# Planning a whole kernel with the scheduler's detailed time model, with TensorE held to the order of the source

## The chip, the cores and the metric

The kernel runs on one core of a Trainium2 chip. The metric is the device time of one execution in microseconds (us), lower is better. The core has five engines that work beside each other, each of which takes its own instructions in a fixed order: TensorE (PE, with its weight loads shown as PEld), VectorE (DVE), ScalarE (ACT), GpSimd (POOL) and SyncE (SP, which only issues DMAs). ACT and POOL issue some DMAs too.

## What is computed

One layer of an encoder on 2048 tokens of width 1024: a gated linear attention mixer (GLA), then a feed-forward network with a short causal convolution, each behind an RMS norm and with a residual sum, and a last RMS norm.

```python
def gla_mixer(h, w_in, w_gate2, b_gate, norm_w, w_out):
    q, k, v, r, glr = split(h @ w_in)                  # 4 heads, dk 128, dv 256, gate rank 16
    log_a = log_sigmoid(glr @ w_gate2 + b_gate) / 16
    g = cumsum(log_a within chunks of 64); g_end = g[:, :, -1]
    k_dec = k * exp(g_end - g)
    # over the chunks: state = state * exp(g_end) + k_dec^T v ;  o = q state
    o = rms_normalize(o) * norm_w * silu(r)
    return o @ w_out

def conv_ffn(h, w_up, conv_w, conv_b, w_down):
    u = causal_dwconv(h @ w_up, conv_w, conv_b)        # 3 taps, 2 x 2816 channels
    g, val = split(u, 2)
    return (silu(g) * val) @ w_down

def reference(x, ...):
    x = x + gla_mixer(rmsnorm(x, mix_norm_w), ...)
    x = x + conv_ffn(rmsnorm(x, ffn_norm_w), ...)
    return rmsnorm(x, final_norm_w)
```

## The kernel before

**Arithmetic.** Everything is fp32 at full precision: each operand is split into a rounded part and a rest (`split`: ACT makes `hi` at line 193, DVE makes `lo` at line 194), and each product takes three matmuls of 128x128 weights against 512 columns (`mm3p`, lines 184 to 186). Each large matrix product is done in seven block products p1 to p7 instead of eight (a Strassen-Winograd scheme), which is why sums and differences of blocks are made, stored to HBM and read again.

**Stages.** They follow one another in the source:

- R, A, B: the input projections, in 8 pairs of token tiles each (`unit`). R makes the gate r and the gates' pre-activations; A and B make q, k, v of two heads each. The gates (`gates`, lines 606 to 654) run beside R and the beginning of A: a pre-activation, softplus, split, a prefix sum by matmul (`pd`, line 639), an exponential on ACT (line 640), a store, and a transpose of the result on TensorE (`pe`, line 631). The scan over chunks runs in slots between the products of A and B and at the beginning of Y: `scan_f` (transposes `pq`, silu of r at line 714), `scan_k` (state update, `pk`), `scan_o` (`po`, then the normalized row `og` at line 763), `scan_x` (transposes `px` of og, line 771).
- Y: the mixer's output projection, the residual sum, the second norm, and the transposes of its rows, h2 (`blocks`, `pt_d`, line 840).
- The up-projection with convolution (`phase_u`): 2 halves of the tokens, each with 11 groups of two channel tiles and all seven products. POOL forms weight sums (lines 1274 to 1292), ACT and DVE split them (`uw`), TensorE multiplies (`ua`, `ub`, `uc`), ACT copies results out of PSUM (`c`, lines 1297 and 1411), ACT and DVE do the convolution (lines 1313 and 1315), and the results go to HBM. h_p are the split operands, read from HBM as `hz` (first half) and `hd` (second half).
- The down-projection: 7 products in 2 halves (`pd_p`, weights `dw`, activations `da` read from HBM), the last sums and the norm.

**What sets the order.** The source is one straight program of 15,608 traced instructions, counting pool markers. It emits work in an order that its author has laid out: a small clock in the program (`adv`, `later_do`) places the preparation of later products, the gates, the scan and the transposes among the products of the present one, with delays such as TB0 to TB3 in microseconds. After that the compiler's planner orders each engine's instructions: it runs the program on a model of the chip and, whenever an engine is free in that model, gives it the earliest instruction in source order among those that the model has ready. An engine's order therefore differs from the source's wherever the model has an earlier instruction waiting. Buffers are rotating slots of fixed number; an instruction that writes a slot waits for the slot's last reader. A few order edges are written by hand (`issue_after`): they hold an instruction behind another one of the same engine, without a wait for its end.

```python
    def mm3p(ps_ap, pairs, first=True, last=True, more=False, mid=None):
        for i, ((ah, al), (bh, bl)) in enumerate(pairs):
            nc.tensor.matmul(ps_ap, ah, bl, start=(first and i == 0), stop=False, **kw)   # 184
            nc.tensor.matmul(ps_ap, al, bh, start=False, stop=False, **kw)                # 185
            nc.tensor.matmul(ps_ap, ah, bh, start=False, stop=..., **kw)                  # 186
            adv(3 * 0.227 * ps_ap.free_size() / 512)
            ...
    def split(hi, lo, src):
        order["act"] = nc.scalar.copy(hi, src)                                            # 193
        nc.vector.tensor_sub(lo, src, f32(hi))                                            # 194
```

Other lines that the profile names: 461 multiplies the transposed input `xt` by the norm's weight (`hb`) on DVE; 1069, 1154 and 1211 take projection results out of PSUM (`cp` is the ACT copy of the first product of a bank); 226 and 828 belong to the second norm (`var_d`, the store of `x1d`).

Of the kernel before, what the change touches and what calls it, by code (L numbers as in the profile page):

```python
# [22 lines left out]


@with_exitstack
def hybrid_kernel(
    ctx: ExitStack,
    tc: tile.TileContext,
    x: bass.AP,
# [1607 lines left out]
            use(o, s, m, banks[m], nwf)  # L1637


_INS = [  # L1640
    "x", "xt", "mix_norm_w", "ffn_norm_w", "final_norm_w",
    "gla_w_in", "gla_w_gate2", "gla_b_gate", "gla_norm_w", "gla_w_out",
# [35 lines left out]
```

## Time and profile before

| | us |
|---|---|
| median of 3 runs | 2118.95 (2118.75 to 2119.75) |
| the profiled execution's own time | 2119.17 |
| its span, first to last instruction | 2117.5 |
| PE busy | 2049.1 |
| DVE busy | 1605.2 |
| ACT busy | 1109.4 |
| POOL busy | 672.5 |

The mean granted clock of TensorE is 0.994. A busy time is the union of an engine's instructions; matmuls overlap a little in it, since one record is about 0.39 us long while the next begins after about 0.23 us. An engine's idle time before an instruction is put down to whatever ended it; idle time matters where it holds up the engine that bounds a stage. Times in rows count from the start of the span.

### The profile page before, as it was taken

How to read it: one execution, taken by the hardware profiler on the slowest of the kernel's cores; microseconds unless marked ns; L12 is line 12 of the kernel's file. 1: busy time of each engine (PE TensorE's matmuls, PEld its weight loads, DVE VectorE, ACT ScalarE, POOL GpSimd, SP SyncE). 2: the span in 40 equal slices, each digit the busy share in tenths (PEclk: the TensorE clock that was granted, in tenths of full speed). 3: DMA queues.
4: the chain of work that ended last, by engine and by line, in shares of the span. 5: the costliest groups of instructions: out<-in, count | busy, mean ns of one | idle time of the engine just before them, and what ended most of it. 6: DMA issues, size and time to landing. Idle time of an engine off the chain costs nothing.

```text
span 2117.5 us, 28200 instructions
## 1 busy us (share of the span) xinstructions
PE 2049.1 (97%) x9700; PEld 1686.1 (80%) x9700; DVE 1605.2 (76%) x2109; ACT 1109.4 (52%) x2022; POOL 672.5 (32%) x595
## 2 busy tenths in 40 slices
PE   6999999999998998999999999999999999999998
PEld 4777778878886887888888887888888788888886
DVE  7766887888878646899898867898898956566564
ACT  5656755675665666655545545445454533233342
POOL 2110000000000002555464554666766433243310
PEclk9999999999999999999999999999999999999999
DMA  8866675577858888444545376545445684454462
GB/s 293 295 219 199 223 237 178 165 247 254 292 183 267 314 271 293 155 159 136 182 139 167 132 278 204 140 110 152 122 129 148 196 322 155 144 179 164 148 218 112
DMA packets 246512, 419.32 MB, mean 198 GB/s; under 512 B 22784, under 2 KB 91520, under 8 KB 246368
## 3 DMA queue, kind: packets, MB, share of 16 engines
q1 hardware_dynamic: 203200, 335.09, 46.5%
q10 hardware_dynamic: 36832, 70.89, 9.8%
q0 software_dynamic: 6336, 11.54, 3.5%
q8 instruction: 76, 1.25, 0.2%
q14 instruction: 68, 0.56, 0.1%
HBM read 278.50 MB, written 150.47 MB: 203 GB/s over the span
## 4 chain that ended last, share of the span: by engine, by line
PE 64%; DVE 13%; POOL 7%; issue 7%; DMA 7%; ACT 2%; SPq 0%; ACTq 0%; DVEq 0%; POOLq 0%
PE pd_p L184 7%; PE pd_p L186 7%; PE pd_p L185 7%; DVE t L1315 4%; PE ua L185 4%; PE ua L184 4%; PE ua L186 3%; POOL as_p L1344 3%; DVE uw_p L194 3%; PE mp_A L184 2%; PE mp_Y L184 2%; PE mp_Y L185 2%; PE mp_Y L186 2%; PE mp_A L185 2%; PE mp_A L186 2%
## 5 line engine op out<-in xcount | busy, mean ns | idle before, releaser
L184 PE MATMUL ua<-h_p,uw_p 128*128 128x512 f32 x704 | 276.9, 393 | 10.2 <-ACT c L1297 4.5
L185 PE MATMUL ua<-h_p,uw_p 128*128 128x512 f32 x704 | 276.0, 392 | 2.8 <-DVE var_d L226 2.8
L186 PE MATMUL ua<-h_p,uw_p 128*128 128x512 f32 x704 | 275.5, 391 | 0.0
L1315 DVE SCALAR_TENSOR_TENSOR t<-u,cw,t 128x1024 f32<-128x1024 f32 x176 | 265.6, 1512 | 8.5 <-ACT t L1313 7.8
L184 PE MATMUL pd_p<-dw_p,da 128*128 128x512 f32 x616 | 239.6, 389 | 0.0
L185 PE MATMUL pd_p<-dw_p,da 128*128 128x512 f32 x616 | 239.6, 389 | 0.0
L186 PE MATMUL pd_p<-dw_p,da 128*128 128x512 f32 x616 | 239.6, 389 | 0.0
L193 ACT CAST uw_p<-us 128x512 fp32r<-128x512 f32 x132 | 82.2, 622 | 198.8 <-POOL us L1277 138.3
L194 DVE TENSOR_TENSOR da<-da_p,da 128x512 fp32r<-128x512 f32 x154 | 118.9, 826 | 87.9 <-ACT da L193 87.9
L194 DVE TENSOR_TENSOR uw_p<-us,uw_p 128x512 fp32r<-128x512 f32 x132 | 153.3, 1166 | 42.4 <-ACT uw_p L193 37.7
L194 DVE TENSOR_TENSOR uw_p<-ur,uw_p 128x512 fp32r<-128x512 f32 x176 | 146.3, 860 | 28.1 <-ACT uw_p L193 28.1
L184 PEld LDWEIGHTS ua<-h_p,uw_p 128*128 128x128 f32 x704 | 133.0, 189 | 43.2 <-ACT c L1297 8.9
L193 ACT CAST da<-da_p 128x512 fp32r<-128x512 f32 x154 | 84.7, 618 | 150.4 <-PE pd_p L186 115.3
L185 PEld LDWEIGHTS ua<-h_p,uw_p 128*128 128x128 f32 x704 | 133.0, 189 | 30.6 <-DVE uw_p L194 3.4
L186 PEld LDWEIGHTS ua<-h_p,uw_p 128*128 128x128 f32 x704 | 133.2, 189 | 27.9
L760 POOL TENSOR_TENSOR rstd<-var,pair 128x2 f32<-128x2 f32 x32 | 22.7, 709 | 410.7 <-DVE var L759 410.7
L184 PE MATMUL uc<-h_p,uw_p 128*128 128x512 f32 x352 | 137.1, 390 | 1.2 <-DMA h_p<-hd_p 1.2
L186 PE MATMUL uc<-h_p,uw_p 128*128 128x512 f32 x352 | 137.0, 389 | 0.0
L185 PE MATMUL uc<-h_p,uw_p 128*128 128x512 f32 x352 | 136.9, 389 | 0.0
L1313 ACT ACTIVATE t<-u,cw 128x1024 f32<-128x1024 f32 x88 | 109.6, 1245 | 49.9 <-DVE u L1424 49.1
L186 PEld LDWEIGHTS pd_p<-dw_p,da 128*128 128x128 f32 x616 | 115.6, 188 | 24.1
L185 PEld LDWEIGHTS pd_p<-dw_p,da 128*128 128x128 f32 x616 | 115.6, 188 | 24.1
(263 smaller groups left out, 5287.3 us busy)
## 6 DMA issues: line engine op xcount, KB each, us to landing
ur<-in_ffn_w_up_dram SPq DMA_DIRECT2D x84, 512.0 KB, 5.2
da_p<-ad_p SPq DMA_DIRECT2D x154, 256.0 KB, 4.1
ad_p<-t SPq DMA_DIRECT2D x110, 256.0 KB, 3.1
ch<-in_ffn_w_down_dram SPq DMA_DIRECT2D x61, 256.0 KB, 4.9
hr_A_p<-h1d_p SPq DMA_DIRECT2D x56, 256.0 KB, 3.3
hr_B_p<-h1d_p SPq DMA_DIRECT2D x56, 256.0 KB, 3.2
hr_Y_p<-yd_p SPq DMA_DIRECT2D x56, 256.0 KB, 3.9
hd_p<-h2p_p ACTq DMA_DIRECT2D x56, 256.0 KB, 2.1
```

Of the source, the lines that this page charges most:

```text
L184: nc.tensor.matmul(ps_ap, ah, bl, start=(first and i == 0), stop=False, **kw)
L185: nc.tensor.matmul(ps_ap, al, bh, start=False, stop=False, **kw)
L186: nc.tensor.matmul(ps_ap, ah, bh, start=False, stop=(last and i == len(pairs) - 1), **kw)
L193: order["act"] = nc.scalar.copy(hi, src)
L194: nc.vector.tensor_sub(lo, src, f32(hi))
L760: nc.gpsimd.tensor_tensor(rstd, var, neghalf.to_broadcast([P, 2]), op=ALU.pow)
L1313: nc.scalar.activation(t, u[:, 2:2 + TS], AF.Identity, scale=cw[:, 2, c:c + 1], bias=cw[:, 3, c:c + 1])
L1315: nc.vector.scalar_tensor_tensor(t, u[:, k:k + TS], cw[:, k, c:c + 1], t, op0=ALU.mult, op1=ALU.add)
L1344: upool["ins"] = nc.gpsimd.tensor_add(av, last if x is None else x, y)
```

## The change

The body of the kernel is renamed, and a new outer function runs all of it inside one block of the tile context. The block is to be planned with the compiler's more detailed model of the chip's timing instead of the usual one, and inside it TensorE is set to manual scheduling: its instructions keep the order of the source, and the planner chooses only for the other engines and their DMA queues. No instruction of the body, no buffer and no hand-written order edge is touched.

```diff
 @with_exitstack
-def hybrid_kernel(
+def body(
     ctx: ExitStack,
     tc: tile.TileContext,
     x: bass.AP,
...
             use(o, s, m, banks[m], nwf)
 
 
+def hybrid_kernel(tc, *args):
+    with tc.block(schedule_with_timeline_sim=True):
+        with tc.manual_schedule(engines={mybir.EngineType.PE}):
+            body(tc, *args)
+
+
 _INS = [
```

## Prediction

> **What bounds the kernel now.** I read the page first, then the stretches by stage, then what TensorE (PE) waits for, and last the order of time around each of its long waits.
>
> ```profile
> span 2117.5 us, 28200 instructions
> PE 2049.1 (97%) x9700; PEld 1686.1 (80%) x9700; DVE 1605.2 (76%) x2109; ACT 1109.4 (52%) x2022; POOL 672.5 (32%) x595
> ...
> 25.00:295.00 270.00, 256.49 (x1359) 207.01 (x1358) 200.86 (x304) 173.22 (x334) 34.74 (x56) 1.00 0.72 239
> 295.00:660.00 365.00, 349.89 (x1936) 290.24 (x1935) 295.35 (x572) 225.62 (x498) 19.75 (x28) 0.99 0.68 226
> ...
> 870.00:1210.00 340.00, 338.90 (x1494) 280.09 (x1493) 304.41 (x311) 179.51 (x274) 169.46 (x141) 1.00 0.47 156
> 1300.00:1660.00 360.00, 357.45 (x1569) 293.48 (x1568) 317.54 (x281) 178.09 (x263) 243.28 (x187) 1.00 0.47 127
> 1720.00:2090.00 370.00, 370.00 (x1634) 306.39 (x1633) 217.84 (x285) 128.03 (x232) 107.31 (x80) 1.00 0.53 184
> ```
>
> After each stretch's length come the busy times of PE, PEld, DVE, ACT and POOL, then granted clock, DMA share and GB/s. The matmuls are the bound: PE is idle for 2117.5 - 2049.1 = 68.4 us in all. The up-projection (870 to 1210, 1300 to 1660) leaves it 1.1 and 2.6 us idle, the down-projection none. The idle time lies in the mixer's stages, 13.5 us (25 to 295) and 15.1 us (295 to 660), and at the head, the two seams of the feed-forward part and the tail. No instruction's work changes, so a new order can win at most that idle time and the halved clock that follows some of it.
>
> Four places show a fault of order: an engine that takes its instructions in order stands at one whose input has not come, with ready work for PE behind it. A row has start, length, engine, line, operation and tiles, and in brackets the engine's idle time and what ended it. The landing row is that of tile xt in the first 16 us; a row with an arrow from engine to engine gives a wait's total, count and longest.
>
> ```profile
> 8.99 2.50 DVE L194 TENSOR_TENSOR w_R_p<-ws_p,w_R_p 128x1024 fp32r<-128x1024 f32 x2 [7.31 <-ACT w_R_p L193]
> DMA to landing us min/median/max: 2.8/6.6/8.0
> 12.93 1.29 DVE L461 TENSOR_TENSOR hb<-xt,nwt 128x512 f32<-128x512 f32 x2
> 14.73 0.79 PE L184 MATMUL m_R<-w_R_p,h_R 128*128 128x512 f32 x1 [14.73 <-ACT h_R L193]
> ...
> 311.87 0.63 ACT L714 ACTIVATE r<-r 128x512 f32<-128x512 f32 x1 [3.25 <-DMA r<-rd]
> 312.40 0.67 ACT L1211 ACTIVATE cp_A<-mp_A,rs 128x512 f32<-128x512 f32 x1
> 313.13 0.51 PE L184 MATMUL mp_A<-w_A_p,h_A_p 128*128 128x512 f32 x1 [1.95 <-ACT cp_A L1211]
> ...
> PE mp_A L184 <- ACT cp_A L1211: 2.7, 3, 1.9
> ...
> 828.38 2.23 ACT L193 CAST h_p<-h_p 128x1024 fp32r<-128x1024 f32 x2 [0.56 <-DMA h_p<-hz_p]
> 830.52 1.13 ACT L193 CAST uw_p<-ur 128x512 fp32r<-128x512 f32 x2
> 831.18 1.02 PE L184 MATMUL ua<-h_p,uw_p 128*128 128x512 f32 x2 [3.09 <-ACT uw_p L193]
> 834.97 0.79 PE L185 MATMUL ua<-h_p,uw_p 128*128 128x512 f32 x1 [2.77 <-DVE var_d L226]
> ...
> 1670.81 0.62 ACT L193 CAST da<-da_p 128x512 fp32r<-128x512 f32 x1 [1.05 <-DMA da_p<-ad_p]
> ...
> 1671.96 0.61 PE L184 MATMUL ua<-h_p,uw_p 128*128 128x512 f32 x1 [2.48 <-ACT c L1411]
> ```
>
> At 311.87 ACT waited 3.25 us for a gate row; the copy that frees PE's bank (cp_A) stood behind it. At 828 and 1670 it is the same with h_p and da. The planner must have expected those landings sooner. There are three waits for cp_A, 2.7 us in all.
>
> **The change part by part.**
>
> *The block* adds a jump at either end for every engine; nothing hides the first. No row shows its price. The nearest is what now lies around the span for entry and exit, 2119.17 - 2117.5 = 1.7 us; I bound it by 0 and that and take the middle, 0.8.
>
> *TensorE held to the source's order.* I set the matmuls in the order in which the source emits them against their order in the trace: 395 of 9700 stand elsewhere, in 20 places, nearly all where the gates end and the scan begins (226 to 256 us), where stages B and Y begin, and at the transposes of h2. At each the planner let ready products go ahead of an operation whose input was late; pinned, PE waits there.
>
> ```profile
> 238.11 0.39 PE L184 MATMUL mp_A<-w_A_p,h_A_p 128*128 128x512 f32 x1
> ...
> 240.31 0.66 PE L631 MATMUL pe<-ident,e 128*128 128x128 f32 x4
> ...
> 242.68 0.39 PE L639 MATMUL pd<-ll,later 128*128 128x512 f32 x1
> ...
> 244.42 0.48 PE L639 MATMUL pd<-ll,later 128*128 128x512 f32 x1
> ...
> 248.41 0.66 PE L631 MATMUL pe<-ident,e 128*128 128x128 f32 x4
> 248.82 0.48 PE L639 MATMUL pd<-ll,later 128*128 128x512 f32 x1
> ...
> 250.76 0.60 PE L631 MATMUL pe<-ident,e 128*128 128x128 f32 x4
> ...
> 428.91 0.39 PE L184 MATMUL mp_B<-w_B_p,h_B_p 128*128 128x512 f32 x1
> ...
> 432.19 0.41 PE L771 MATMUL px<-ident,og 128*128 128x128 f32 x2
> ...
> 642.41 0.39 PE L184 MATMUL mp_Y<-w_Y_p,h_Y_p 128*128 128x512 f32 x1
> ...
> 646.23 0.41 PE L771 MATMUL px<-ident,og 128*128 128x128 f32 x2 [0.93 <-DVE og L763]
> ...
> 658.89 0.90 PE L771 MATMUL px<-ident,og 128*128 128x128 f32 x3 [4.91 <-DVE og L763]
> ```
>
> Scan start: the source puts the pe of 240.31 where the product of 238.11 stands, so PE waits 2.2 us; then pd (242.68) follows at once instead of behind six products, some 1.7 more. Later pe, pd, pe stand together, and each pe needs the exponential of the pd before it: 3.9 us from 244.42 to 248.41 as now, 1.9 from 248.82 to 250.76 at best; less what lies between, 1.2 to 3.9 and 1.3 to 1.9. Sum 6.4 to 9.7; I take 8.0, most of the way up, since these latencies belong to ACT and DVE.
>
> What absorbs part of the rest, and what idle time costs in clock:
>
> ```profile
> 310.70:317.20 6.50, 4.55 (x14) 3.25 (x13) 4.53 (x9) 3.68 (x8) 0.00 (x0) 0.74 0.52 190
> 827.70:840.00 12.30, 6.42 (x17) 4.37 (x16) 8.72 (x11) 7.87 (x12) 6.76 (x5) 0.72 1.01 409
> PE mp_B L185 <- DVE h_B_p L194: 2.0, 2, 1.8
> PE px L771 <- DVE og L763: 7.0, 3, 4.9
> PE mp_Y L185 <- DVE h_Y_p L194: 1.4, 1, 1.4
> ```
>
> Start of B: the transpose px moves from behind eleven products to ahead of them: 432.19 - 428.91 = 3.3 us, against the wait of 1.8 and the third px wait (7.0 - 4.9 - 0.9 = 1.2), both within the next 25 us, which a later PE no longer meets: +0.3. Start of Y: 646.23 - 642.41 = 3.8, less the 0.9 there, the 1.4 behind it, and 2.7 of the 4.9 at 658.89, which twelve products now fill (12 x 370/1634 us, the pace of the down-projection): -1.2. The h2 transposes pass seven products in one place and six in another, 1.6 + 1.4 = 3.0. A later PE asks nothing of SP's or POOL's queues.
>
> Around the 1.95 us wait at 313 the granted clock is 0.74 over 6.5 us, so (1 - 0.74) x 6.5 = 1.7 us of matmul are lost; around the seam at 831 it is 0.28 x 12.3 = 3.4. So one new long wait (scan start) adds 1.7; those at B and Y replace ones that stand there now. Pins together: 8.0 + 1.7 + 0.3 - 1.2 + 3.0 = 11.8. The low bound is 0 (with the new plan the inputs come in time), the high one 26, with nothing absorbed (9.7 + 3.4 clock, 3.3 + 1.7, 3.8 + 1.7, 3.0).
>
> The Trainium skill, "TensorE: Matmul & The Clock Gate", section "HAM oscillation — how this bites in real kernels", puts the limit for idle gaps at about 3.4 us. The trace disagrees: 1.95 us of idle were followed by a lowered clock. By that rule the scan-start waits, none of them above 3.4 us in a piece but one, would cost little clock and the repair at 313 would win none; the two cancel in the sum.
>
> *The other four queues planned by the finer model.* DVE, ACT, POOL and SP keep every instruction, DMA and hand-written order edge (those of issue_after); only the choice among ready work changes. If the finer model has landings as late as the trace, ready work goes first:
> - Head: DVE's hb needs only an xt, whose loads are among the first DMAs and took 2.8 to 8.0 us to land, yet ran at 12.93, behind two w_R_p. With hb earlier the first product could start when w_R_p ends, 11.5, not 14.73. Win 0 to 3.2; I take 2, since the weights still come by DMA.
> - Stage A: the waits for cp_A, 2.7, with the 1.7 of clock: 4.4.
> - Seam to the up-projection: 3.09 + 2.77 + 3.4 of clock = 9.3; DVE must still split h_p, so 6.
> - Seam to the down-projection: 2.48, and 1.7 of clock as after the similar wait at 313: 4.2.
> - Short waits left in the mixer: 28.6 us of idle (25 to 660) less 2.7 (A), 3.0 (B) and 7.2 (Y) leave 15.7; bounds +16 and -16, since an order can lose as much as it wins. I take -5, nearer nothing.
>
> Together 2 + 4.4 + 6 + 4.2 + 5 = 21.6. SP's issues move too (1086 DMAs); it is no bound. Twelve table loads of 1.28 us on ACT can become a few more, beside PE's work at 52% busy.
>
> **The sum**, against the profiled execution's own 2119.17 us (span 2117.5; 0.01% above the median 2118.95): 2119.2 + 0.8 + 11.8 - 21.6 = 2110.2; I say 2110.
>
> **The rivals.**
>
> *VectorE falls behind in the up-projection* (slower).
>
> ```profile
> L194 DVE TENSOR_TENSOR uw_p<-us,uw_p 128x512 fp32r<-128x512 f32 x132 | 153.3, 1166 | 42.4 <-ACT uw_p L193 37.7
> L194 DVE TENSOR_TENSOR uw_p<-ur,uw_p 128x512 fp32r<-128x512 f32 x176 | 146.3, 860 | 28.1 <-ACT uw_p L193 28.1
> ```
>
> DVE is busy 304.4 of 340 us and 317.5 of 360; the work comes in 22 groups of some 38 us, each with 4.0 to 4.5 us of DVE slack. The same split takes 1166 or 860 ns, and DVE waits 65.8 us (37.7 + 28.1) for ACT's halves, 3.0 a group. If a new order brought the 176 to 1166 ns (2.4 a group) and doubled that wait (3.0), it would pass the slack by 1.2 us: 22 x 1.2 = 26, or 2145 with the pins and repairs cancelling. It decides from 4 us a group; against it, the finer plan has no reason to favour waiting. 15%.
>
> *The pins cost what they cost and the queues barely change* (slower): 2119.2 + 0.8 + 11.8 = 2132. For it: the planner is greedy and gives nothing a preference for PE's sake. 20%.
>
> *Nothing measurable*: the new orders differ only where slack covers it, or wins equal the pins: 2119 within 4 us (0.2%, about what a measurement of this kernel can tell from no change). 18%.
>
> *All repairs and all the short waits, pins free*: 2119.2 + 0.8 - 3.2 - 4.4 - 9.3 - 4.2 - 16 = 2083. 7%.
>
> **How the numbers follow.** My forecast's case, 2095 to 2115, has 40%. Faster by over 0.2%: 40 + 7 = 47%; within: 18%; slower: 20 + 15 = 35%. The range reaches from the full repair, 2086, to the VectorE rival, 2146; beyond lie some 6% below and 12% above.
>
> **What would show it.** Right: the first product before 14 us; no wait of cp_A, uw_p or c at 313, 831 and 1671; new waits for pe and px at the starts of A and B; DVE idle in the up-projection as now, near 10%. Wrong: PE idle there above 3 us a stretch, or the short mixer waits grown past 16 us.

## The result: slower by 0.5%

| | before | changed |
|---|---|---|
| median of six runs beside each other, us | 2119.35 (2118.11 to 2121.88) | 2130.54 (2125.50 to 2135.39) |
| the profiled execution, its span, us | 2119.17, 2117.5 | 2129.33, 2127.6 |
| mean granted clock of TensorE | 0.994 | 0.986 |

The ratio is 1.0050, with a 95% interval of 1.0035 to 1.0066: slower, where 2110 was forecast. The page of the changed kernel begins:

```profile
span 2127.6 us, 28302 instructions
PE 2055.0 (97%) x9700; PEld 1698.0 (80%) x9700; DVE 1590.6 (75%) x2109; ACT 1113.2 (52%) x2021; POOL 678.0 (32%) x595
```

TensorE's idle time is 72.6 us against 68.4, which is 4.2 of the 10.1 us by which the span grew. The rest is in the busy time, which grew by 5.9 us for the same 9700 matmuls, at a granted clock of 0.986 instead of 0.994: idle time has been paid for a second time by the clock. The stretches (columns as in the prediction) show where:

```profile
25.00:295.00 270.00, 254.61 (x1323) 206.21 (x1323) 193.47 (x282) 166.88 (x322) 31.12 (x55) 0.97 0.70 234
295.00:660.00 365.00, 348.28 (x1909) 291.29 (x1910) 291.12 (x562) 222.51 (x485) 18.49 (x27) 0.97 0.66 219
870.00:1210.00 340.00, 338.65 (x1494) 279.80 (x1495) 287.92 (x312) 185.53 (x287) 168.83 (x143) 1.00 0.48 155
1300.00:1660.00 360.00, 360.00 (x1590) 298.10 (x1589) 319.97 (x281) 177.57 (x263) 247.07 (x186) 1.00 0.52 136
```

In the mixer (first two rows) the granted clock fell from 1.00 and 0.99 to 0.97: fewer matmuls fit into the same time, 1323 and 1909 against 1359 and 1936. The second half of the up-projection (last row) has no idle time left, and 1590 matmuls instead of 1569. So the change lost in the mixer and won in the feed-forward part. What TensorE waits for now:

```profile
PE po L184 <- DVE sl L194: 14.5, 4, 4.5
PE m_R L184 <- DVE w_R_p L194: 10.2, 1, 10.2
PE pg L568 <- DVE wg L528: 8.1, 1, 8.1
PE pe L631 <- ACT e L640: 6.4, 5, 3.0
PE pt_d L840 <- ACT h L831: 6.2, 4, 2.9
PE px L771 <- DVE og L763: 3.3, 1, 3.3
...
PE mp_A L184 <- ACT cp_A L1211: 0.8, 1, 0.8
```

The largest is one that the kernel before did not have: `po`, the product of q with the state in the scan, waits for `sl`, the rest of the split state. The rows of one such wait, from the timelines of VectorE, ScalarE and TensorE:

```profile
423.63 0.87 DVE L739 SCALAR_TENSOR_TENSOR state<-state,dec,pk 128x256 f32<-128x256 f32 x2
...
427.62 0.68 DVE L194 TENSOR_TENSOR h_B_p<-hr_B_p,h_B_p 128x512 fp32r<-128x512 f32 x1
428.21 0.74 DVE L1154 SCALAR_TENSOR_TENSOR o_A<-mp_A,rs,cp_A 128x512 f32<-128x512 f32 x1
428.88 0.48 DVE L702 SCALAR_TENSOR_TENSOR kd<-E,pair,o_A 128x256 f32<-128x256 f32 x1
429.27 1.22 DVE L194 TENSOR_TENSOR w_B_p<-wr_B,w_B_p 128x1024 fp32r<-128x1024 f32 x1
430.40 0.69 DVE L194 TENSOR_TENSOR sl<-state,sh 128x512 fp32r<-128x512 f32 x1
...
424.99 0.63 ACT L193 CAST h_B_p<-hr_B_p 128x512 fp32r<-128x512 f32 x1
426.01 1.05 ACT L193 CAST w_B_p<-wr_B 128x1024 fp32r<-128x1024 f32 x1 [0.39 <-DMA wr_B<-in_gla_w_in_dram]
426.96 0.61 ACT L193 CAST sh<-state 128x512 fp32r<-128x512 f32 x1
...
426.69 0.28 PE L184 MATMUL po<-sl,q 128*128 128x256 f32 x1
426.81 0.28 PE L185 MATMUL po<-sh,q 128*128 128x256 f32 x1
426.93 0.28 PE L186 MATMUL po<-sh,q 128*128 128x256 f32 x1
431.14 0.58 PE L184 MATMUL po<-sl,q 128*128 128x256 f32 x1 [3.94 <-DVE sl L194]
431.52 0.41 PE L185 MATMUL po<-sh,q 128*128 128x256 f32 x1
431.73 0.41 PE L186 MATMUL po<-sh,q 128*128 128x256 f32 x1
```

The state is done at 424.50. Its rounded part `sh` begins 2.5 us later, behind two casts for stage B on ScalarE; the rest `sl` begins 2.8 us after `sh` is done, behind four instructions on VectorE, all of which come later in the source. TensorE stands for 3.94 us, and then goes slower: its `po` matmuls begin 0.12 us apart ahead of the wait, and 0.21 apart behind it (431.52 to 431.73).

**The same matmul in two traces.** Each matmul can be found in both traces by its number in the source. How much later it starts than in the kernel before, in us (median over the matmuls within 3 us of the place in the first column, which is a time of the kernel before; the other columns are the experiments below):

```
   at  block_only pin_only changed old_line scan_usual scan_pin late_model
   24     -0.2      +1.3     +4.3    +4.4      +4.2      +4.6     +0.3
   75     +3.6      +1.1     +2.2    +3.1      +3.8      +3.5     +3.5
  222     +5.6      +0.5     -1.9    +1.1      +1.1      -0.1     -1.0
  275     +5.5     +11.9     +9.9    +3.6      +4.4     +10.2     -1.0
  420     +3.1     +13.4     +5.1    -1.2      +0.4      +5.5     -2.2
  600     +3.0     +14.9    +18.2   +12.4      -0.9      +6.6     -3.7
  720     +2.4     +18.3    +22.2   +18.3      -1.9     +10.7     -5.5
  917     +2.4     +20.0    +22.8   +19.2      -1.9      +9.9     -5.9
 1600     +3.8     +20.5    +16.7   +13.2      -7.9      +3.9    -11.9
 1700     -0.1     +20.1    +10.6    +7.1     -14.0      -2.2    -18.0
 2080     +1.3     +20.5    +10.6    +7.1     -14.0      -2.2    -18.0
```

block_only has the orders of the kernel before on every engine; its column shows what one execution differs from another by, up to 5.6 us, nearly all of it picked up in stage R.

### The profile page after: what moved, and what is told of

Its sections match the earlier page's. It is cut to its first block, busy times and chain, and to the rows that moved or that the text cites. A ratio compares the mean times of both kernels' runs of the same rounds, so it can differ in the third digit from the quotient of the medians.

```text
span 2127.6 us, 28302 instructions
## 1 busy us (share of the span) xinstructions
PE 2055.0 (97%) x9700; PEld 1698.0 (80%) x9700; DVE 1590.6 (75%) x2109; ACT 1113.2 (52%) x2021; POOL 678.0 (32%) x595
## 4 chain that ended last, share of the span: by engine, by line
PE 86%; DMA 6%; ACT 4%; DVE 2%; issue 1%; ACTq 0%; SPq 0%; POOL 0%; DVEq 0%; POOLq 0%
PE ua L184 7%; PE ua L186 7%; PE ua L185 7%; PE pd_p L185 7%; PE pd_p L186 7%; PE pd_p L184 7%; PE uc L186 4%; PE uc L184 4%; PE uc L185 4%; PE mp_Y L184 2%; PE mp_Y L185 2%; PE mp_Y L186 2%; PE mp_A L184 2%; PE mp_A L186 2%; PE mp_A L185 2%; PE ub L184 2%
## 5 line engine op out<-in xcount | busy, mean ns | idle before, releaser
L1315 DVE SCALAR_TENSOR_TENSOR t<-u,cw,t 128x1024 f32<-128x1024 f32 x176 | 257.0, 1472 | 7.6 <-ACT t L1313 7.1
L194 DVE TENSOR_TENSOR uw_p<-ur,uw_p 128x512 fp32r<-128x512 f32 x176 | 158.9, 916 | 36.5 <-ACT uw_p L193 36.5
```

What stands on the lines that cost most here:

```text
L1315: nc.vector.scalar_tensor_tensor(t, u[:, k:k + TS], cw[:, k, c:c + 1], t, op0=ALU.mult, op1=ALU.add)
```

## The experiments

### The three parts by themselves

```diff
-    with tc.block(schedule_with_timeline_sim=True):
-        with tc.manual_schedule(engines={mybir.EngineType.PE}):
-            body(tc, *args)
+    with tc.block():                                              # block_only
+        body(tc, *args)
...
+    with tc.block():                                              # pin_only
+        with tc.manual_schedule(engines={mybir.EngineType.PE}):
+            body(tc, *args)
...
+    with tc.block(schedule_with_timeline_sim=True):               # model_only
+        body(tc, *args)
```

**block_only.** 

> The body in one block, with the usual time model and TensorE left to the planner. Every engine's order is the same as before, so this is the price of the block alone. Theory (the block is nearly free, as the prediction's term of 0.8 says): 2119 to 2121 us. Rival (the block's entry and exit carry the loss of 10 us): 2127 to 2131.

Measured 2118.89 us, ratio 0.9996 (0.9983 to 1.0008). The block costs nothing that can be measured, and the rival is out.

**pin_only.** 

> The block with the usual time model, and TensorE held to the source's order: the pin without the finer model. Theory (the pin is what costs: TensorE stands at the starts of the scan, of B and of Y, and the halved clock after each such wait doubles the price; matmul by matmul the changed kernel falls behind by 11.6 us from 220 to 260, 7.8 from 430 to 470, 5.3 at 550 and 4 from 650 to 720, 28.7 in all): 2140 to 2148. The prediction's price of the pins, 11.8, would give 2132. Rival (the late inputs come from the finer model's order on VectorE and ScalarE, and the pin alone is harmless): 2117 to 2123, with waits of pe at 248 and px at 555 as short as before.

Measured 2136.93 us, ratio 1.0081 (1.0065 to 1.0097): 17 us. My 28.7 was too much, since it booked to the pin what the changed kernel loses in the scan, and the time stayed under the 2140 to 2148 that went with it; the prediction's 11.8 was too little; the harmless pin is out. Its waits:

```profile
PE pe L631 <- ACT e L640: 9.6, 5, 3.3
PE px L771 <- DVE og L763: 8.5, 3, 3.6
PE mp_A L184 <- ACT cp_A L1211: 6.4, 3, 2.8
PE mp_Y L184 <- DVE x L1199: 5.4, 1, 5.4
```

From 222 to 275 us it falls behind by 11.4 us (scan start), and by 5.1 between 600 and 917 (stage Y and the h2 transposes). There is no long `po` wait.

**model_only.** 

> The block with the finer time model, and TensorE left to the planner: the model without the pin. Theory (the model's repairs are real, some 24 us in the lags of the changed kernel: 6 in stage R, 4.7 in A, 1.6 and 11.9 in the feed-forward part; against them stand 10 at the head, where the gate weights come late, and 2 at the seam to the up-projection; the pins' 28.7 go): 2103 to 2111. Rival (late inputs come from the finer model's order itself): 2122 to 2132, no better than the changed kernel.

Measured 2131.69 us, ratio 1.0056 (1.0041 to 1.0072). Without the pin the finer model is slow too, as the rival had it (2122 to 2132). That is not idle time: TensorE is idle for only 57.2 us (span 2129.1, busy 2071.9), while its busy time grew by 22.8 us. The groups of `pk`, the state update, are the first two rows of the kernel before, then of model_only:

```profile
L732 PE MATMUL pk<-vh,kz 64*128 64x256 f32 x256 | 24.3, 279 | 0.0
L732 PE MATMUL pk<-vl,kz 64*128 64x256 f32 x128 | 21.4, 330 | 0.0
...
L732 PE MATMUL pk<-vh,kz 64*128 64x256 f32 x256 | 42.0, 282 | 0.0
L732 PE MATMUL pk<-vl,kz 64*128 64x256 f32 x128 | 36.0, 333 | 4.2 <-ACT ot L800 4.2
```

One matmul is as long as ever (279 and 282 ns), but their union is not: the two of a pair use the upper and the lower 64 rows, and as neighbours they run beside each other. In the kernel before all 192 pairs are neighbours, in model_only 59. From start to start, idle time left out, all 384 take 29.4 us before and 50.5 in model_only. That they run side by side agrees with the Trainium skill, "TensorE: Matmul & The Clock Gate", section "The mechanism" (under packing small matmuls), which says so for matmuls in different row groups.

**pk_pairs** follows this up.

```diff
+        for group in held_back:            # the 12 pk of one state update
+            ... a chain of order edges through the 12, and
+            ... an edge from the last of them to each of the next 60 matmuls of the source
```

> The finer model with TensorE left to the planner, as in model_only, but with the twelve matmuls of each state update (pk) chained in order and the next 60 matmuls of the source held behind them. Theory (model_only loses on TensorE itself: its 384 pk matmuls take 50.5 us against 29.4 before, since the two of a pair, which use the upper and the lower half of the rows and run beside each other when they are neighbours, stand apart in 133 of 192 pairs): pk back at 29 to 31 us, and the run at 2109 to 2114, faster than before. Rival (the loss of model_only comes from late inputs, as its 7.4 us wait at 873 us suggests): pk back at 30, but 2122 to 2131, since longer waits take its place.

Measured 2135.29 us, ratio 1.0080 (1.0063 to 1.0096), above both ranges. 185 of 192 pairs are neighbours again, the unions fall to 28.2 and 26.1 us, and from start to start the 384 take 34.3. But the 60 held matmuls bring waits that were not there:

```profile
L738 PE MATMUL pk<-vh,kz 64*128 64x256 f32 x256 | 28.2, 294 | 0.2 <-DVE kz L198 0.2
...
PE px L778 <- DVE og L770: 29.2, 3, 14.3
```

That the lost pairs lengthen TensorE's busy time is shown by both runs; that model_only would be faster with them is not, because the edit brought 29.2 us of `px` waits.

### The head

```diff
+        order["wg"] = nc.vector.tensor_sub(wg[:, :, RANK:GR], gv, f32(wg[:, :, :RANK]))
...
+        with tc.issue_after(order["wg"].ins):
             weight("p3", (1, 0))           # and the first sums of sum5 and sum6 alike
```

**gate_first.** 

> The changed kernel with hand-written order edges on VectorE in the first pair of token tiles: the split of the gate weights (wg) stands ahead of the first sums and of the split of the second weight block. Theory (the 8.07 us in which TensorE waits for wg at 15.8 us, and the halved clock behind it, are a loss of the whole program, 10 us in the lags): 2120 to 2123. Rival (a TensorE that is earlier there only waits longer for the scan's inputs, which VectorE sets): 2126 to 2130.

Measured 2129.67 us, ratio 1.0045 (1.0030 to 1.0061), against the changed kernel's 1.0050: nothing won, and my theory falls. The wait did go, but what it won is gone by 75 us. Its TensorE and ScalarE rows:

```profile
15.56 0.31 PE L568 MATMUL pg<-h_R,wg 128*32 128x128 f32 x1
...
56.42 0.69 ACT L1214 ACTIVATE cp_R<-mp_R,rs 128x512 f32<-128x512 f32 x1 [4.06 <-POOL rs L441]
```

At 24 us gate_first is 9.2 us ahead of the changed kernel, at 75 us 1.0 behind. ScalarE's copy `cp_R` waits for `rs`, the norm of a row of x, which comes after a load and a sum of squares. In this trace the head is paced by those rows: neither an early first product nor the late `wg` counts for the end. The rival's time came, but not by its mechanism, since the lead is gone long before the scan.

### Two models by two orders of TensorE

In old_line the finer model plans four engines and TensorE has the order of the kernel before.

```diff
+MOVED = ((1052, 1064, 5), (1057, 1052, 12), ...)   # place, number in the source, count
...
+        for place, n, count in MOVED:
+            line[place:place + count] = pe[n:n + count]
+        ... and an order edge from each matmul of line to the next
```

**old_line.** 

> The finer time model for the four other engines, and TensorE held, by order edges, to exactly the order that it has in the kernel before (395 of 9700 matmuls stand elsewhere than in the source). With the kernel before, pin_only and the changed kernel this fills a table of two models by two orders of TensorE. Theory (the parts add: the source's order costs some 17 us whichever model plans the rest, the finer model wins some 6): 2110 to 2115 us, faster than before by 0.2 to 0.45%, with no wait of more than 3 us at 248 us. Rival (the finer model's order on VectorE and ScalarE is late for the scan whatever TensorE does): 2118 to 2126, with the po waits of 14.5 us in all still there.

Measured 2129.48 us, ratio 1.0051 (1.0035 to 1.0067). The rival held in its mechanism, and the time is above even its range: the scan start is good again (+2.5 from 222 to 275 us, against +11.8), yet the time is that of the changed kernel. The finer model has a loss of its own that needs no pin:

```profile
PE po L201 <- DVE sl L211: 20.1, 7, 5.1
```

**pin_gates_free.** The pin with the usual model, but for the gates' matmuls. 

> The usual time model, with TensorE held to the source's order but for the gates' matmuls and transposes (pz, pd, pe), which the planner may place freely; 48 places differ from pin_only's. Theory (the pin's largest cost is the scan start, 11.8 us of lag between 236 and 270 us in pin_only, made of waits for exponentials and of halved clock behind them): 2124 to 2128, some 10 under pin_only's 2137. Rival (whatever is won there is lost again at the starts of B and Y, which wait for the same chain): 2132 to 2138.

Measured 2133.82 us, ratio 1.0073 (1.0061 to 1.0085). The intervals of this run and pin_only overlap; some 4 of the 11 us at the scan start went in the profiled execution, and the `cp_A` waits of stage A grew to 8.4 us. The rival's range of 2132 to 2138 held: what is won there is mostly lost again, but in A rather than at B and Y.

### Where the finer model loses, and where it wins

A list of order edges holds chosen engines to a given order over a part of the source:

```diff
+    for name, spans in LINES:                         # an engine, and its instructions' numbers
+        own = [i for i in traced if i.engine == getattr(mybir.EngineType, name)]
+        line = [own[k] for first, count in spans for k in range(first, first + count)]
+        for a, b in zip(line, line[1:]):
+            tc.add_manual_dep(b, a.name, behind, reason="order")
```

**late_model.** 

> The finer model, with TensorE held to the order of the kernel before throughout, and the four other engines held to the order of the kernel before up to the first instruction of the up-projection (which stands at 830 us). Theory (the finer model's gain is real but lies in the feed-forward part alone: from 917 us to 1683 us the changed kernel, gate_first and old_line all win 12 us on the kernel before, and every loss lies ahead of it): 2106 to 2111 us, faster than before by 0.4 to 0.6%. Rival (those 12 us are only the catching up of a kernel that comes late: the kernel before has idle time there because its loads and sums are just in time, and one that is 20 us late finds them ready): 2115 to 2120, no difference.

**scan_usual.** 

> As old_line (finer model, TensorE in the order of the kernel before), with VectorE and ScalarE alone held to the order of the kernel before from the end of stage A to the first instruction of the up-projection (some 420 to 830 us). Theory (the order that the finer model gives these two makes the state's split, sl, late, 20.1 us of waits in old_line; it is not the DMA queues): the po waits fall under 4 us, the lag of 14.5 us that old_line takes on between 427 and 727 us goes, and the run comes to 2112 to 2117. Rival (their inputs are late, by landings that the queues of SP set, or by TensorE itself): po waits or new waits of more than 10 us in their place, and 2123 to 2130.

late_model measured 2100.80 us, ratio 0.9925 (0.9909 to 0.9942); scan_usual 2103.95, ratio 0.9932 (0.9917 to 0.9948). Both beat both kernels, and both theories were too modest; in scan_usual's stretch no `po` wait is left. The same 3402 matmuls of the feed-forward part in the kernel before, the changed kernel and late_model:

```profile
917.00:1700.00 783.00, 775.81 (x3402) 638.58 (x3401) 679.17 (x658) 400.54 (x600) 439.44 (x355) 1.00 0.52 159
...
939.80:1710.60 770.80, 770.80 (x3402) 638.27 (x3401) 669.72 (x656) 401.90 (x599) 446.94 (x353) 1.00 0.54 161
...
911.10:1682.00 770.90, 770.90 (x3403) 638.73 (x3402) 659.40 (x657) 401.89 (x599) 446.52 (x354) 1.00 0.53 161
```

783.0 us became 770.8, with no idle time at all. The gain is 12.1 or 12.2 us in the changed kernel, old_line, scan_usual, scan_pin and late_model alike, whether the kernel arrives there 23 us late or 6 early, while with the usual model pin_only, 20 us late, wins nothing and block_only 2.5. It is not a catching up. In late_model it is 12.1 of the 18.0 us by which the profiled execution leads; the rest lies in the mixer, where its orders are those of the kernel before, and is about what block_only shows two executions to differ by (5.6). The gain by the medians is 17 us, with an interval of 12.3 to 19.3. And the same 1554 matmuls between 420 and 720 us, in the kernel before, old_line and scan_usual:

```profile
420.00:720.00 300.00, 286.05 (x1554) 236.53 (x1553) 245.27 (x462) 190.29 (x418) 17.45 (x25) 0.99 0.75 254
...
418.80:738.30 319.50, 293.84 (x1554) 244.17 (x1554) 245.86 (x463) 190.84 (x416) 17.45 (x25) 0.95 0.72 242
...
420.40:718.10 297.70, 286.73 (x1554) 237.53 (x1553) 245.36 (x462) 190.60 (x418) 17.44 (x25) 0.98 0.77 260
```

With the finer model's order on VectorE and ScalarE the stretch takes 319.5 us, with the usual order on these two 297.7. All else was planned by the finer model in both, so the orders on these two engines set off the loss. That the DMA queues have no part in it is not shown: ScalarE itself issues some 30 DMAs in this stretch, and the plan for SP's queue changed with the two engines (61 of the 218 DMAs that both traces have there change places). Of the 21.8 us, 14.7 are idle time (25.7 against 11.0) and 7.1 are busy time at a clock of 0.95 against 0.98.

### Which of the two engines, and the pin's own price

dve_usual and act_usual hold one of the two engines; scan_pin has TensorE in the source's order, and holds the two engines to the order that they have in pin_only.

**act_usual.** 

> As scan_usual, but ScalarE alone is held between 420 and 830 us; VectorE has the finer model's order. Theory (both delay the chain): 2112 to 2120. Rival (VectorE alone decides): 2125 to 2131, as in old_line.

**dve_usual.** 

> As scan_usual, but VectorE alone is held between 420 and 830 us; ScalarE has the finer model's order. Theory (both engines delay the state chain: in the changed kernel the rounded part sh begins 2.5 us after its state is done, behind two casts on ScalarE, and the rest sl 2.8 us after sh, behind four instructions on VectorE): about half of scan_usual's 25 us, 2112 to 2120. Rival (VectorE alone decides, since its queue is the fuller one): 2103 to 2108.

**scan_pin.** 

> The changed kernel (finer model, TensorE in the source's order), with VectorE and ScalarE alone held, from the end of stage A to the first instruction of the up-projection, to the order that the usual model gives them when TensorE is pinned (that of pin_only). Against scan_usual it shows the price of the source's order once those two engines are in time. Theory (the pin's price is its own, 17 us as with the usual model, and was hidden in the changed kernel behind inputs that came late anyway): 2117 to 2123. Rival (under the finer model the source's order costs next to nothing, as old_line and the changed kernel, 2129.5 and 2130.5, suggest): 2103 to 2108.

| | us | ratio to before |
|---|---|---|
| old_line, neither held | 2129.48 | 1.0051 (1.0035 to 1.0067) |
| dve_usual | 2122.51 | 1.0022 (1.0007 to 1.0037) |
| act_usual | 2111.24 | 0.9968 (0.9952 to 0.9984) |
| scan_usual, both | 2103.95 | 0.9932 (0.9917 to 0.9948) |
| scan_pin, both, source's order | 2116.66 | 0.9995 (0.9982 to 1.0008) |

Each engine delays the chain by itself: holding VectorE wins 7 us, ScalarE 18, both 25.5, and the parts add. That VectorE alone decides is out. Against the theory's range of 2112 to 2120 for either, act_usual came out a little better and dve_usual 2.5 us worse: the two are not worth the same. The `po` waits fell to 2.9 us in act_usual and 2.4 in dve_usual, and waits for `og`, the last step of the same chain, took their place. The first row is act_usual's, the second dve_usual's, then scan_pin's:

```profile
PE px L803 <- DVE og L795: 12.5, 6, 6.2
...
PE px L804 <- DVE og L796: 10.1, 6, 4.3
...
PE px L810 <- DVE og L802: 8.6, 3, 3.6
PE mp_Y L223 <- DVE x L1238: 6.9, 2, 5.6
PE pe L670 <- ACT e L679: 6.1, 5, 2.1
```

scan_pin is 12.7 us slower than scan_usual: the source's order costs about that once the inputs come in time, 17 with the usual model, and only 1 by the medians in the changed kernel over old_line. Why so little there stays open: in the traces the changed kernel loses 9.3 us more than old_line from 222 to 275 us, had 3.0 in hand from stage R, and gets back only 2.8 behind it.

## Why the prediction was wrong, point by point

- **What bounds the kernel** held: matmuls, with the idle time in the mixer and at the seams.
- **The block, +0.8.** block_only: -0.8, within -3.6 and +1.7 by its interval. Right; of the jump that the term was for, the trace shows nothing (28200 instructions, as before).
- **The pins, +11.8.** 12.7 (scan_pin) and 17.4 (pin_only): right for the one, too low for the other, inside the bounds of 0 to 26. The scan start, put at 8.0 and 1.7 of clock, took 11.4 us in pin_only; its clock was mis-sized, as the next point says. B, Y and the h2 transposes, put at 2.1, took 6.6 from 420 to 917 us. The high bound adds up to 26.6, not 26.
- **The clock** was booked once, for one new long wait, 1.7. In the changed kernel the two stretches around the scan start alone lie at 0.86 and 0.69:

```profile
219.70:231.50 11.80, 9.50 (x35) 7.29 (x34) 10.63 (x14) 9.33 (x13) 0.00 (x0) 0.86 0.84 277
245.00:256.00 11.00, 6.80 (x24) 4.91 (x25) 6.30 (x10) 3.62 (x9) 0.10 (x1) 0.69 0.97 355
```

  (1 - 0.86) x 11.8 + (1 - 0.69) x 11.0 = 5.1 us, part of it in idle time. The rule that the prediction weighed, from the Trainium skill ("TensorE: Matmul & The Clock Gate", "HAM oscillation — how this bites in real kernels"), would have little clock lost here, since no piece of idle time in these stretches is above 3.4 us (the longest is 2.98). The trace disagrees once more: the 2.98 us were followed by half clock for 6.8 us. Nor would the two terms of that rule cancel in the sum, as the prediction has it, since the 3.4 and 1.7 us of clock booked at the two seams would have gone as well.
- **The head, -2.** The first product did start at 10.20 us instead of 14.73, and it is worth nothing: gate_first shows that a lead of 9 us at 24 us is gone at 75. The step failed by taking a start for an end.
- **Stage A, -4.4.** `cp_A` waits fell from 2.7 to 0.8 us; from 275 to 420 us the changed kernel and old_line win 4.8. Right in size, though block_only, without the finer model, wins 2.4 there too.
- **The seam to the up-projection, -6.** The waits for `uw_p` and `var_d` are gone, and from 825 to 841 us (times of the kernel before) this wins 7.6 to 8.8 us in the changed kernel, old_line, scan_usual and late_model (block_only loses 0.1). By 860 us they have lost 5.9 to 10.2 again: late_model, which has no lag to make up, wins only 0.4 from 720 to 917 us. New waits took their place, for the h2 transposes (`pt_d`) and for the copy `c`. In late_model they are:

```profile
834.42 1.97 PE L912 MATMUL pt_d<-ident,h 128*128 128x128 f32 x8 [3.88 <-ACT h L903]
850.45 0.50 PE L256 MATMUL ua<-h_p,uw_p 128*128 128x512 f32 x1 [1.95 <-ACT c L1369]
```

  So the wait itself was priced about right, and its worth at the end was wrong, by the same error as at the head.
- **The seam to the down-projection, -4.2.** From 1600 to 1700 us every kernel with the finer model wins 6.1; block_only, without it, wins 3.9 there, so the wait varies by itself. Right as far as that goes; but a further 6.0 to 6.1 won between 917 and 1600 us (block_only loses 1.4 there), short waits for `c` and for h_p, were not in the sum at all.
- **Short waits left in the mixer, -5, with bounds of 16 either way.** This is the step that failed. I took the finer model to have waits where the trace has them, and so to be nearer to the chip everywhere. The -5 stands on nothing else. Over the stretch that it was read from, 25 to 660 us, the same matmuls take 648.7 us in old_line against 635.0: 13.7 more, the win in stage A included, of which 5.3 are idle time and 8.4 busy time at a clock of 0.97 against 0.99. In the stretch from 420 to 720 us old_line loses 19.5 us on the kernel before, and scan_usual wins 2.3: the order on VectorE and ScalarE costs 21.8 us in the traces and 25.5 in the medians. I saw no wait for `sl` in the kernel before and asked only which waits would go, not which chains with slack would lose it. The bounds of 16 counted waits alone, while idle time here costs clock as well: 14.7 idle, 7.1 clock.

In old_line's profiled execution the stretches add up: +1.1 up to 222 us, +2.5 to 275, -4.8 to 420, +19.5 to 720, +0.9 to 917 and -12.1 behind it, together +7.1; its median is +10.7, and by the medians the pin adds 1. So the loss in the scan is larger than all that the finer model repairs. The changed kernel's 2130.5 lies inside the range of 2086 to 2146, but that range was wide enough for either sign. (Its low end was to be the full repair, which the prediction's own sum puts at 2083.) Of the rivals, "the pins cost what they cost and the queues barely change" gave the nearest time, 2132, by luck: the queues changed much, both ways. VectorE did not fall behind in the up-projection: its idle share is 15% and 11%, against some 10 and 12 before. Of the signs named, the first product and the three repaired waits came as said; `pe` has its new waits, but at the start of B it is `po` and not `px` that waits.

Why the finer model puts `sh` and `sl` so late was not tried. What two places show is that it puts the reader of a fresh result behind later work: between the two halves of `wg` (lines 527 and 528) stand eight instructions in the changed kernel and one before, and ahead of `sl`, in the rows above, four that come later in the source.

## What to carry to other kernels

A planner's model is to be judged stretch by stretch: in this kernel the same model won 12 us where independent work streams past TensorE and lost 25 us where a chain over three engines (`pk`, state, `sh`, `sl`, `po`) has to come round in time. Split such a change by parts and by stages before giving it up: the orders of the finer model in the feed-forward part alone make a kernel of 2100.80 us, 0.75% faster than before (0.58 to 0.91%). When a forecast counts waits that will go, it should list the chains that have slack now, and ask what each costs if the new order spends it; and it should ask whether an earlier start lasts, which at the head and at the up-projection it did not.

## What the runs showed of the hardware

Two matmuls of 64 rows by 256 columns on different halves of the rows ran beside each other only as neighbours in TensorE's order: their starts lie 0.00 to 0.01 us apart in all 192 pairs of the kernel before. With 133 pairs apart, in model_only, the 384 of them cost 21.1 us more (50.5 against 29.4).

The clock follows shorter waits than I had expected. Take from 14 traces the waits of TensorE between 60 and 2050 us that stand alone (no more than 0.6 us of other idle time from 10 us before the wait's start to 6 us after it) and begin at full clock. Of some 100 waits between 0.2 and 1.5 us none was followed by half clock within 5.2 us of its start, of 35 between 1.5 and 2.3 us 11 were, and of 39 between 2.3 and 6 us 35 were. The half clock lasted 3.4 us or a multiple of it, and 3.4 us at half clock lose up to 1.7 us of work. Of the 13 waits between 2.3 and 3 us, ten were followed by 3.4 us of it, one by 6.8 and two by none. Several of the traces share their orders, so these are not all independent cases.
